# A hybrid decoder layer on one Trainium2 core: the embedding projection goes between output projection and FFN, the kernel begins with the gate rows and the first columns by token halves, and the first FFN pair is computed by seven products too

## The chip, the cores and the metric

One NeuronCore of a Trainium2 chip runs the whole layer. The engines that matter here are TensorE (PE, with its weight loads PEld beside it), VectorE (DVE), ScalarE (ACT) and GpSimd (POOL); SyncE (SP) and ACT issue the DMAs. The metric is device time per execution in microseconds (us); lower is better.

## The reference

One layer on 1,024 tokens, width 1,024, everything float32:

```python
u = RMSNorm(x)
y = u @ w_in              # columns of three token mixers and of the merge gates
# A: gated DeltaNet, 4 heads (conv, decay, delta rule); B: mLSTM, 4 heads; C: native sparse attention, 8 heads
h = x + (sum_i sigmoid(gate_i(u)) * (mixer_i(y) @ w_branch[i])) @ w_out
r = h + (silu(n @ w_gate) * (n @ w_up)) @ w_down        # n = RMSNorm(h), 2,816 hidden channels
out = r + sigmoid(RMSNorm(r) @ w_ple_gate) * (p @ w_ple_proj)   # p: 256 values per token
```

Among the columns of `w_in` are 40 that give one scalar per head and token (decay, write strength, input and forget gate of A and B, the branch gates of C). They are called the gate rows below.

## The kernel before

**Precision.** A float32 product is three fp32r matmuls: each factor is split into `hi` (a rounding copy, by ACT) and `lo` (the rest, by DVE or POOL), and hi\*hi, hi\*lo and lo\*hi are summed in PSUM. So each weight has `whi` and `wlo`, the normed input `uhi`/`ulo`, the FFN's input `u2hi`/`u2lo`.

**Blocks.** `run_blocks` goes through a list of weight blocks of up to 1 MB (four tiles of 128x512) on TensorE. In the middle of block i, `following` issues the split of block i+1 (`halve`) and, on SP, the load of block i+2. There are four raw buffers and five of each split half, so a split of the next block can also wait until TensorE has let go of an older one. The scalar and vector work of the mixers runs as generators that are advanced between matmuls; `later(lag, ...)` puts a step that many microseconds of TensorE work further on. Every engine runs its instructions in one fixed order.

**Start.** A warm-up of 48 transposes, then the projection of p: 16 transposes `ptr` of p, 96 matmuls 128x512, 16 ACT copies `pp` and 16 stores to DRAM, where p's projection waits for the end of the kernel. Between these matmuls the normed x is transposed (`trx`, 64) and split into `uhi`, `ulo` (L320, L321). Then the block of the gate rows, 32 matmuls, then the gated DeltaNet's first head: query and key columns (96 matmuls), value and output-gate columns. The gate rows are transposed (`gtr`), and a chain of small steps makes the decays of A and the stabiliser of B from them (L653 on).

**Middle.** The rest of the in-projection beside the mixers' scans, attention, then the branch projections, which end in `merged`.

**Out projection** (`out_blocks`): eight blocks (token half, quarter of 256 columns), each row tile 24 matmuls with 256 moving columns; after the fourth quarter of a row tile `norm_after` normalises it, and `to_u2` transposes it into `u2hi`/`u2lo` (eight 128x128 pieces).

**FFN.** The 2,816 hidden channels are 11 pairs of 256. Pair 0 is done plainly: `gate` and `up` with 96 matmuls each, then `down(0)` with 96. Pairs 1 to 10 are done by seven products in place of eight (`seven(f)`): a gate and an up tile of 128 channels, as a 2x2 block matrix over channel kind and half of the width, times the 2x2 input over width and token half. That needs sums of weights (`sums`, DVE) and four sums of inputs T1 to T4. `ffn_combine(k)`, k = 0 to 3, makes the latter, each with 12 DVE operations of 128x512 (`uw` sums, `utT..l` remainders) and four ACT copies `utT..h`; they are due 8 us of TensorE work apart, behind the last `norm_after`.

**Gate at the end** (`ple_blocks`): like the out projection, 768 matmuls of 256 columns.

Of the kernel before, what the change touches and what calls it, by code (L numbers as in the profile page):

```python
# [11 lines left out]
F32 = mybir.dt.float32  # L12
F32R = mybir.dt.float32r
# [20 lines left out]
NORM_AT = [1, 3]  # L34
TRX_AT = [0, 0, 1, 1, 3, 3, 4, 4, 7, 8, 9, 10, 11, 12, 13, 14]
FOLLOW_AT = 12
CONST_AT = 2
# [23 lines left out]
def _constants():  # L61
# [44 lines left out]
    add("rowscale", np.where((m % 64 >= 4) & (m % 64 < 8), -1.0, 1.0))  # L106
# [30 lines left out]
def _blocks(w_in, w_branch, w_out, w_ffn_in, w_ffn_out, w_ple_gate, w_ple_proj):  # L137
# [5 lines left out]
    out.append(w_ple_proj.reshape(2, P, 2, 512).transpose(1, 2, 0, 3).reshape(P, -1))  # L143
    rows = np.zeros((D, 256), w_in.dtype)
    for dst, src, n in ((0, 2048, 4), (4, 4108, 4), (8, 2052, 4), (12, 4104, 4), (16, 5392, 24)):
        rows[:, dst:dst + n] = rows[:, 64 + dst:64 + dst + n] = w_in[:, src:src + n]
    cols(rows, (0, 256))
# [21 lines left out]
    for c in range(4):  # L169
        cols(w_out, (256 * c, 256))  # L170
    for i in range(NFP):
        if i == 0:
            cols(w_ffn_in, (0, 256))
            cols(w_ffn_in, (DFF, 256))
        else:
            for c in (256 * i, 256 * i + P):
                g, u = (_rows(w_ffn_in[:, o:o + P]) for o in (c, DFF + c))
                out.append(np.concatenate([t.reshape(P, -1) for t in (g[:, :4], u[:, :4], u[:, 4:], g[:, 4:])], 1))
        out.append(w_ffn_out[256 * i:256 * i + 256].reshape(2, P, 2, 512).transpose(1, 2, 0, 3).reshape(P, -1))
    for c in range(4):  # L180
        cols(w_ple_gate, (256 * c, 256))
# [3 lines left out]
def _layout(x, p, rel_bias, norm_mix, w_in, conv_w, gdn_a_log, gdn_dt_bias, gdn_norm, mlstm_b_i, mlstm_b_f,  # L185
# [17 lines left out]
    chan.append(rb)  # L203
    o["chan"] = np.concatenate(chan, 1)
# [10 lines left out]
       "pe": (74, 64), "rowb": (138, 1)}  # L215
# [12 lines left out]
class Trunk:  # L228
    def __init__(self, ctx, tc, x, p, w, relb, chan, rowp, wcmp, c128, cset, c33, out, dbg=None):
# [169 lines left out]
    def run_blocks(self, blocks, rate, both=0, first=None, fetch=None):  # L399
# [21 lines left out]
        def halve(i):  # L421
            if i < n:
# [4 lines left out]
                for t in parts:  # L427
                    hi = self.wpool.tile([P, 512], F32R, tag="whi", name="whi", bufs=W_BUFS[1])
                    lo = self.wpool.tile([P, 512], F32R, tag="wlo", name="wlo", bufs=W_BUFS[1])
                    nc.scalar.activation(hi, t, AF.Copy)  # L430
                    eng = nc.vector if len(blocks[i]) == 2 and len(self.wsplit[i]) % 2 < both else nc.gpsimd
                    eng.tensor_tensor(lo, t, hi.bitcast(F32), OP.subtract)  # L432
# [1685 lines left out]
```

## Time and profile before

| | |
|---|---|
| median of 3 runs | 2327.62 us (2327.32 to 2328.61) |
| profiled execution: time | 2327.02 us |
| its span | 2325.2 us, mean granted clock 0.994 |
| TensorE busy | 2263.7 us, 97% |
| VectorE, ScalarE, GpSimd busy | 57%, 37%, 31% |

The span is the time between the first and the last instruction that the profiler saw; the 1.8 us between it and the execution's own time is launch and end. TensorE's 3% of idle time is what any wait has cost; the rest is matmuls, transposes and their clock. The projection of p, which the table does not show apart, is among the first 62 us.

### The profile page before, as it was taken

Reading aid. Unit: us, or ns where it says so; the run is one execution under the profiler, and the core shown is the slowest. Engines: PE = TensorE matmul, PEld = TensorE weight load, DVE = VectorE, ACT = ScalarE, POOL = GpSimd, SP = SyncE. Lnnn points to the kernel's source line nnn. Section 1 sums busy time; section 2 is a strip of 40 time slices with the busy share of each in tenths; the row PEclk is TensorE's granted clock in tenths of the full one; section 3 lists DMA queues with packets and bytes.
Section 4 is the critical chain, followed back from the end, with each engine's and each line's share of the span. In section 5 each row is a group of like instructions: output and inputs, shape, how many; then the busy total and the mean of one; then the engine's idle time right before and its main releaser. Section 6 shows DMA issues by size and latency. Waiting matters only on the chain.

```text
span 2325.2 us, 34431 instructions
## 1 busy us (share of the span) xinstructions
PE 2263.7 (97%) x12800; PEld 1836.2 (79%) x12800; DVE 1332.0 (57%) x3096; ACT 852.3 (37%) x1832; POOL 729.1 (31%) x616
## 2 busy tenths in 40 slices
PE   7999999999999999999999999999999999999999
PEld 6777878788778996677667778987888888888899
DVE  6456564645223446888883456586555555555594
ACT  6423232423332335555553222453222222222362
POOL 2343334433231123322122151214334444344411
PEclk9999999999999999999999999999999999999999
DMA  6131312111222132111103553311111111111144
GB/s 235 47 104 37 98 37 89 58 50 52 82 69 75 47 111 87 64 46 37 46 33 130 199 183 122 119 55 46 55 50 51 51 54 50 50 50 55 55 139 130
DMA packets 121887, 183.05 MB, mean 79 GB/s; under 512 B 25275, under 2 KB 47204, under 8 KB 121720
## 3 DMA queue, kind: packets, MB, share of 16 engines
q1 hardware_dynamic: 121432, 180.72, 23.6%
q8 instruction: 101, 1.65, 0.3%
q14 instruction: 66, 0.54, 0.1%
q10 hardware_dynamic: 288, 0.14, 0.0%
HBM read 149.04 MB, written 31.76 MB: 78 GB/s over the span
## 4 chain that ended last, share of the span: by engine, by line
PE 84%; DVE 10%; issue 2%; ACT 2%; DMA 1%; POOL 1%; SPq 0%; ACTq 0%; POOLq 0%; DVEq 0%
PE mm L243 68%; PE nso L243 3%; PE ptr L251 2%; PE S L243 2%; DVE P L1525 1%; PE mops L243 1%; PE gks L243 1%; PE gram L243 1%; PE gpu L243 1%; DVE P L1514 1%; POOL wlo L432 0%; DVE uw L1825 0%; DVE kT L824 0%; DVE xn L1778 0%; PE u2tr L251 0%
## 5 line engine op out<-in xcount | busy, mean ns | idle before, releaser
L432 POOL TENSOR_TENSOR wlo<-wraw,whi 128x512 fp32r<-128x512 f32 x334 | 443.8, 1335 | 1021.8 <-ACT whi L430 790.0
L243 PE MATMUL mm<-u,whi 128*128 128x512 f32 x1888 | 628.5, 408 | 3.6 <-ACT mg L1654 2.0
L430 ACT ACTIVATE whi<-wraw 128x512 fp32r<-128x512 f32 x408 | 255.8, 630 | 417.3 <-PE mm L243 335.7
L243 PEld LDWEIGHTS mm<-u,whi 128*128 128x128 f32 x1888 | 345.1, 190 | 76.8 <-issue 5.2
L243 PE MATMUL mm<-u,wlo 128*128 128x512 f32 x928 | 374.2, 403 | 3.1 <-POOL wlo L432 3.1
L243 PEld LDWEIGHTS mm<-u,wlo 128*128 128x128 f32 x928 | 175.8, 189 | 41.0 <-POOL wlo L432 3.5
L1896 DVE TENSOR_TENSOR fc<-fc,mm 128x512 f32<-128x512 f32 x140 | 95.2, 686 | 156.1 <-PE mm L243 156.1
L1937 DVE TENSOR_TENSOR h<-h,mm 128x512 f32<-128x512 f32 x176 | 118.6, 684 | 58.6 <-PE mm L243 57.3
L243 PE MATMUL mm<-whi,ahi 128*128 128x512 f32 x352 | 140.2, 398 | 2.0 <-ACT utT4h L1819 2.0
L243 PE MATMUL mm<-whi,alo 128*128 128x512 f32 x352 | 141.4, 402 | 0.0
L243 PE MATMUL mm<-wlo,ahi 128*128 128x512 f32 x352 | 140.2, 398 | 0.0
L432 POOL TENSOR_TENSOR wlo<-ws,whi 128x512 fp32r<-128x512 f32 x60 | 85.0, 1416 | 153.6 <-ACT whi L430 153.6
L243 PE MATMUL mm<-u2hi,whi 128*128 128x512 f32 x304 | 121.2, 399 | 0.0
L243 PE MATMUL mm<-u2lo,whi 128*128 128x512 f32 x304 | 120.9, 398 | 0.0
L243 PE MATMUL mm<-u2hi,wlo 128*128 128x512 f32 x304 | 120.4, 396 | 0.0
L1520 ACT ACTIVATE P<-P,n_ng 128x640 f32<-128x640 f32 (+7 forms) x128 | 92.8, 727 | 53.5 <-DVE n_ng L1518 53.0
L430 ACT ACTIVATE whi<-ws 128x512 fp32r<-128x512 f32 x60 | 37.8, 630 | 171.4 <-DVE h L1937 126.1
L251 PE MATMUL ptr<-ident,P 128*128 128x128 f32 x528 | 88.6, 281 | 8.2 <-DVE P L1525 7.5
L243 PE MATMUL mm<-whi,u 128*128 128x256 f32 x512 | 94.2, 283 | 0.0
L251 PEld LDWEIGHTS ptr<-ident,P 128*128 128x128 f32 x528 | 60.8, 141 | 40.4 <-DVE P L1525 13.1
L432 DVE TENSOR_TENSOR wlo<-wraw,whi 128x512 fp32r<-128x512 f32 x74 | 64.5, 871 | 46.0 <-ACT whi L430 46.0
L243 PEld LDWEIGHTS mm<-whi,alo 128*128 128x128 f32 x352 | 66.6, 189 | 18.8 <-DVE alo L1853 3.2
(506 smaller groups left out, 4995.2 us busy)
## 6 DMA issues: line engine op xcount, KB each, us to landing
wraw<-in_w_dram SPq DMA_DIRECT2D x408, 256.0 KB, 2.6
mgs<-mg SPq DMA_DIRECT2D x48, 256.0 KB, 2.2
mgld<-mgs SPq DMA_DIRECT2D x48, 256.0 KB, 5.4
xt<-in_x_dram SPq DMA_DIRECT2D x8, 512.0 KB, 6.0
xt<-in_x_dram SPq DMA_DIRECT2D x32, 128.0 KB, 3.4
sg<-pps SPq DMA_DIRECT2D x32, 128.0 KB, 3.3
out_dram<-sg SPq DMA_DIRECT2D x32, 128.0 KB, 2.4
pps<-ppst SPq DMA_DIRECT2D x8, 256.0 KB, 2.0
```

The source lines that it names most:

```text
L243: return self.nc.tensor.matmul(out, lhsT, rhs, start=start, stop=stop).ins
L251: self.nc.tensor.transpose(out, in_, self.ident[:n, :n])
L430: nc.scalar.activation(hi, t, AF.Copy)
L432: eng.tensor_tensor(lo, t, hi.bitcast(F32), OP.subtract)
L1514: nc.vector.tensor_tensor_reduce(pt[:, farw:nk], sp2[:, farw - cut:nk - cut], near[g][:, n % 2], 1.0, -3e38, OP.add, OP.max, mx[:, n, 1:2])
L1520: nc.scalar.activation(pts[i][:, :nk], pts[i][:, :nk], AF.Exp, bias=ng[:, i:i + 1], accum_out=sm[:, g, i % 2:i % 2 + 1])
L1525: nc.vector.tensor_scalar(pts[i][:, :nk], pts[i][:, :nk], sm[:, g, i % 2:i % 2 + 1], gate[:, g, i % 2:i % 2 + 1], OP.mult, OP.mult)
L1896: nc.vector.tensor_tensor(t, x, ps, OP.add)
L1937: nc.vector.tensor_tensor(self.h[tt][s], self.h[tt][s], ps, OP.add)
```

## The change

**Start.** The projection of p is no longer there, nor the 1 MB weight block of the gate rows: their 40 columns come by a DMA of their own on ACT's queue (`wgr`), are split by ACT and DVE into `wg` (104 columns, hi and lo side by side) and are multiplied in `first_block`, between the transposes of x. That block is the first head's query and key block, ordered by token halves: transposes and gate rows of half 0, query and key columns of half 0, transposes and gate rows of half 1, query and key columns of half 1.

**Out projection and last gate.** `wide_blocks` replaces `tok_block`: the token tile is held, 512 weight columns move; a block is half the width and half the columns, and eight blocks remain. The sum with x is written into x's tile.

**Projection of p.** Its loads (`load_p`) and transposes (`prep_p`) go out with the last out block, its matmuls stand between out projection and FFN, row tile by row tile.

**FFN pair 0.** `first_three(f)` for both f, then `last_four(f)` for both f, then `down(0)`. The weight block of a tile is loaded and split twice, once for each part. Three of the seven products need no T: B11, B21, B22 are plain pieces of the input.

**End.** The last tile's gate is finished in two halves.

```diff
+    def wide_blocks(self, u, evac, key, then=None):
...
+                    for k, (wh, wl) in enumerate(wb):
+                        uh, ul = u(4 * kh + k, tt)
+                        self.mm(ps, uh, wh, kh == 0 and k == 0, False)
+                        self.mm(ps, uh, wl, False, False)
+                        self.mm(ps, ul, wh, False, kh == 1 and k == 3)
+                    if kh == 1:
+                        evac(c, tt, ps)
+                    if then and kh and c:
+                        then(tt)
+                    self.passed(2.56)
...
+        return [(gen_for(c, kh, _HALF[hf]), (key, c, kh)) for hf in range(2) for c in range(2) for kh in range(2)]
...
-    def gates_block(self):
+    def first_block(self, evac):
...
+            trx(0)
+            trx(0)
+            gate_rows(0, 2)
+            self.norm_x(2)
+            self.norm_x(3)
             for hf in range(2):
...
+                        if hf == 0 and ct == 1 and kc > 4:
+                            trx(1)
...
+                    if hf == 0 and ct == 1:
+                        gate_rows(1, 3)
+                        self.load_gains()
+                        self.flags.add("rows")
+                    if hf == 1 and ct == 0:
+                        self.following()
...
+        def then(tt):
+
+            if tt == 4:
+                self.load_p()
+            elif tt > 5:
+                self.prep_p(tt - 6)
...
+        def sums_b(raw):
+            a11, a21, a22, _ = raw
+            s1, s2 = self.l2("ws1"), self.l2("ws2")
+            nc.vector.tensor_tensor(s1, a21, a22, OP.add)
+            nc.vector.tensor_tensor(s2, s1, a11, OP.subtract)
+            yield s2
...
+        def first_three(f):
+            def gen(wb):
...
+                nc.scalar.activation(c1, product(0, "B11"), AF.Copy)
+                yield
+                g0 = add(c1, product(1, "B21"))
+                nc.scalar.activation(g0, g0, AF.Silu)
+                yield
+                nc.scalar.activation(t7, product(2, "B22"), AF.Copy)
...
+        def last_four(f):
...
+                add(t2, product(0, "T2"), t2)
+                yield
+                t3 = add(t2, product(1, "T3"))
...
+                p5 = product(2, "T1")
...
+                add(t3, product(3, "T4"), t3)
...
             if i == 0:
-                blocks.append((self.chan_block(self.u2c, gate, halves_first=True), None))
-                blocks.append((self.chan_block(self.u2c, up, halves_first=True), None))
+                blocks += [(first_three(f), ("ffn", f), sums_a) for f in range(2)]
+                blocks += [(last_four(f), ("ffn", f), sums_b) for f in range(2)]
...
-                    t = self.s2("pp") if s else self.ppst[tt // 2][:, (tt % 2) * 512:(tt % 2) * 512 + 512]
+                    t = self.l2("pp")
                     nc.scalar.activation(t, ps, AF.Copy)
                     nc.sync.dma_start(self.pp[tt, :, s * 512:s * 512 + 512], t)
...
-                blocks = [(self.ple_proj_block(), None), (self.gates_block(), None)]
+                blocks = []
                 for h in range(4):
-                    blocks += self.gdn_blocks(h)
+                    blocks += self.gdn_blocks(h, h == 0)
```

How this moves instructions shows best in the order of three engines. In these lists a row is one instruction or a run of like ones: line of the file, operation, result and operands, size, count; lines are those of the file before and after, which differ. First TensorE from the program's start, before and then after (`warm`: warm-up, `ptr`: transposes of p, `pThi`/`pTlo`: p's halves, `trx`: transposes of x, `u`: its halves, `wg`: columns of the gate rows):

```order
L251 MATMUL warm<-ident 128x128 x48
L251 MATMUL ptr<-ident,pt 128x128 x16
L243 MATMUL mm<-whi,pThi 128x512
L243 MATMUL mm<-wlo,pThi 128x512
L243 MATMUL mm<-whi,pTlo 128x512
L243 MATMUL mm<-whi,pThi 128x512
L243 MATMUL mm<-wlo,pThi 128x512
L243 MATMUL mm<-whi,pTlo 128x512
L251 MATMUL trx<-ident,xt 128x128 x8
```

```order
L249 MATMUL warm<-ident 128x128 x48
L249 MATMUL trx<-ident,xt 128x128 x12
L241 MATMUL mm<-u,wg 104x512 x2
L249 MATMUL trx<-ident,xt 128x128 x4
L241 MATMUL mm<-u,wg 104x512 x2
```

The transposes of x and the gate rows stand where the projection of p stood. Second, ACT around the combinations, from the last copy of group k = 0 to the first of group k = 2 (`whi`: weight splits, `pp`: copies of p's projection out of PSUM, `sil`: pair 0's gate, `ws`: a sum of weights), before and after:

```order
L1819 ACTIVATE utT4h<-uw 128x512
L430 ACTIVATE whi<-wraw 128x512
L1858 ACTIVATE sil<-mm 128x512 x2
L430 ACTIVATE whi<-wraw 128x512 x2
L1819 ACTIVATE utT1h<-uw 128x512
L1819 ACTIVATE utT3h<-uw 128x512
L1819 ACTIVATE utT2h<-uw 128x512
L1819 ACTIVATE utT4h<-uw 128x512
L1858 ACTIVATE sil<-mm 128x512
L1819 ACTIVATE utT1h<-uw 128x512
```

```order
L1889 ACTIVATE utT4h<-uw 128x512
L2110 ACTIVATE pp<-mm 128x512 x6
L1889 ACTIVATE utT1h<-uw 128x512
L1889 ACTIVATE utT3h<-uw 128x512
L1889 ACTIVATE utT2h<-uw 128x512
L1889 ACTIVATE utT4h<-uw 128x512
L2110 ACTIVATE pp<-mm 128x512 x3
L431 ACTIVATE whi<-wraw 128x512
L2110 ACTIVATE pp<-mm 128x512
L431 ACTIVATE whi<-ws_14692 128x512
L2110 ACTIVATE pp<-mm 128x512 x3
L431 ACTIVATE whi<-wraw 128x512 x2
```

Thirteen of the sixteen copies of p's projection now stand behind the first combination, seven of them and four weight splits between the second and the third (whose `utT1h` is the row that follows). Third, DVE from the end of the last combination (k = 3) on (`h`: sums of the down projection, `alo`: pair 0's activation, `ws`: sums of weights, `fc`: sums of the products), before and after:

```order
L1825 TENSOR_TENSOR uw<-u2hi,u2lo 128x512
L1820 TENSOR_TENSOR utT2l<-uw,utT2h 128x512
L1837 TENSOR_TENSOR uw<-uw 128x512
L1862 TENSOR_TENSOR sil<-sil,mm 128x512
L1937 TENSOR_TENSOR h<-h,mm 128x512
L1820 TENSOR_TENSOR utT4l<-uw,utT4h 128x512
L1937 TENSOR_TENSOR h<-h,mm 128x512
L1853 TENSOR_TENSOR alo<-sil,ahi 128x512
```

```order
L1895 TENSOR_TENSOR uw<-u2hi,u2lo 128x512
L1890 TENSOR_TENSOR utT2l<-uw,utT2h 128x512
L1907 TENSOR_TENSOR uw<-uw 128x512
L1890 TENSOR_TENSOR utT4l<-uw,utT4h 128x512
L1972 TENSOR_TENSOR ws_15102<-wraw 128x512
L1973 TENSOR_TENSOR ws_15103<-ws_15102,wraw 128x512
L1975 TENSOR_TENSOR wraw<-wraw 128x512
L1956 TENSOR_TENSOR fc<-fc,mm 128x512
```

Before, pair 0's own results stand among the combinations; now the weight sums of `last_four(0)`, which the products with T2, T3, T1 and T4 need, stand behind the last of them.

## Rows read from the trace of the kernel before

**Rows 1.** The page's head and its busy times: busy us, share of the span, instructions.

```profile
span 2325.2 us, 34431 instructions
PE 2263.7 (97%) x12800; PEld 1836.2 (79%) x12800; DVE 1332.0 (57%) x3096; ACT 852.3 (37%) x1832; POOL 729.1 (31%) x616
```

**Rows 2.** Busy time by stretch: start and end of the stretch, its length, busy us and instructions of each engine, granted clock, DMA share, GB/s. The stretches are: projection of p and gate rows; rows' transposes and half of the first query and key block; its other half; the rest of the norms and the combinations; the tail of `down(0)`; a piece of the later FFN; the last gate; the tail.

```profile
13.94:62.54 48.60, 42.16 (x209) 33.25 (x209) 29.48 (x63) 30.56 (x54) 11.17 (x13) 0.96 0.60 207
62.54:81.30 18.76, 15.90 (x81) 12.43 (x81) 10.17 (x37) 7.29 (x17) 10.02 (x10) 0.91 0.18 57
81.30:92.50 11.20, 11.20 (x50) 9.04 (x49) 2.48 (x6) 3.94 (x9) 4.45 (x5) 1.00 0.04 12
1526.00:1584.00 58.00, 54.01 (x236) 43.21 (x235) 53.43 (x103) 30.57 (x67) 9.58 (x6) 0.97 0.14 47
1584.00:1601.40 17.40, 17.40 (x70) 13.92 (x69) 13.52 (x20) 1.73 (x3) 2.55 (x2) 0.90 0.09 31
2100.00:2200.00 100.00, 100.00 (x429) 80.08 (x428) 53.42 (x72) 29.79 (x49) 42.31 (x32) 1.00 0.17 56
2255.00:2321.10 66.10, 66.10 (x551) 65.90 (x550) 34.89 (x62) 20.29 (x42) 14.29 (x10) 1.00 0.51 159
```

**Rows 3.** Waits between 1420 and 1600 us, TensorE's: engine, line, what it waited for; us in total, times, longest.

```profile
PE u2tr L251 <- DVE u2lo L321: 3.9, 2, 2.0
PEld mm L243 <- ACT utT4h L1819: 2.5, 1, 2.5
```

**Rows 4.** TensorE by operation between 13.94 and 62.54 us: busy us, mean ns of one (they overlap), idle before and what ended it.

```profile
L251 PE MATMUL trx<-ident,xt 128*128 128x128 f32 x64 | 10.0, 292 | 1.7 <-DVE u L321 1.7
L243 PE MATMUL mm<-u,whi 128*128 128x512 f32 x32 | 8.1, 401 | 1.5 <-ACT pp L1987 1.4 <-DVE whi L628 0.2
L251 PE MATMUL ptr<-ident,pt 128*128 128x128 f32 x16 | 2.8, 288 | 4.0 <-DVE pTlo L318 2.7 <-DMA pt<-in_p_dram 1.3
```

**Rows 5.** Timeline of the start: start us, duration, engine, line, operation, result and operands, count, idle before.

```profile
9.64 1.42 DVE L577 TENSOR_SCALAR xt<-xt,rsq_ynr 128x1024 f32<-128x1024 f32 x2
11.80 4.96 POOL L432 TENSOR_TENSOR wlo<-wraw,whi 128x512 fp32r<-128x512 f32 x4 [10.28 <-ACT whi L430]
13.14 1.19 DVE L297 SCALAR_TENSOR_TENSOR rsq_tnr<-rsq_tnr,nr_ssqx 128x2 f32<-128x2 f32 x1
25.75 1.26 ACT L320 ACTIVATE u<-trx,chan 128x512 fp32r<-128x512 f32 x2
26.46 0.75 DVE L321 SCALAR_TENSOR_TENSOR u<-trx,chan,u 128x512 fp32r<-128x512 f32 x1 [1.53 <-ACT u L320]
```

**Rows 6.** Timeline of the gate rows' chain, the same columns (`gaterows`: their evacuation, `gm`: their transposed values, `mtr`: a transposition of B's chain).

```profile
62.54 0.45 PE L653 MATMUL gtr<-ident,gaterows 40*128 40x40 f32 x8
62.65 0.78 ACT L619 ACTIVATE gaterows<-mm,rowbias,c 104x512 f32<-104x512 f32 x1 [0.25 <-PE mm L243]
67.87 0.23 DVE L670 TENSOR_TENSOR g_tmp<-g_tmp,coef 128x64 f32<-128x64 f32 x1
74.83 0.22 PE L251 MATMUL mtr<-ident,m_crow 32*128 32x32 f32 x1 [2.86 <-DVE m_tmp L737]
```

**Rows 7.** DVE by operation from 1514.75 to 1583.92 us: busy us, mean ns, idle before.

```profile
L1825 DVE TENSOR_TENSOR uw<-u2hi,u2lo 128x512 f32<-128x512 f32 x16 | 12.6, 820 | 0.0
L321 DVE SCALAR_TENSOR_TENSOR u2lo<-u2tr,chan,u2hi 128x128 fp32r<-128x128 f32 x32 | 9.7, 345 | 2.1 <-ACT u2hi L320 2.0
L1760 DVE TENSOR_TENSOR h<-xt,mm 128x256 f32<-128x256 f32 x4 | 1.7, 417 | 0.7 <-PE mm L243 0.7
```

**Rows 8.** Timeline from the out projection's last quarter to the first `seven`, the same columns as rows 5.

```profile
1514.75 0.42 DVE L1760 TENSOR_TENSOR h<-xt,mm 128x256 f32<-128x256 f32 x1 [0.72 <-PE mm L243]
1515.96 0.16 DVE L1775 SCALAR_TENSOR_TENSOR na_ms<-na_ssq 128x1 f32<-128x1 f32 x1 [0.79 <-ACT xn L1773]
1517.69 0.88 DVE L1778 TENSOR_SCALAR xn<-h,rsq_yna 128x512 f32<-128x512 f32 x2
1529.17 2.55 DVE L321 SCALAR_TENSOR_TENSOR u2lo<-u2tr,chan,u2hi 128x128 fp32r<-128x128 f32 x9
1540.06 0.68 DVE L1825 TENSOR_TENSOR uw<-u2hi,u2lo 128x512 f32<-128x512 f32 x1
1548.49 0.63 ACT L430 ACTIVATE whi<-wraw 128x512 fp32r<-128x512 f32 x1 [1.53 <-PE mm L243]
1549.67 1.36 DVE L1820 TENSOR_TENSOR utT4l<-uw,utT4h 128x512 fp32r<-128x512 f32 x1 [0.98 <-ACT utT4h L1819]
1552.14 1.86 POOL L432 TENSOR_TENSOR wlo<-wraw,whi 128x512 fp32r<-128x512 f32 x1 [1.65 <-ACT whi L430]
1552.77 1.78 DVE L1825 TENSOR_TENSOR uw<-u2hi,u2lo 128x512 f32<-128x512 f32 x1
1558.20 0.68 DVE L1825 TENSOR_TENSOR uw<-u2hi,u2lo 128x512 f32<-128x512 f32 x1
1558.80 0.69 DVE L1820 TENSOR_TENSOR utT2l<-uw,utT2h 128x512 fp32r<-128x512 f32 x1
1583.31 0.68 DVE L1820 TENSOR_TENSOR utT4l<-uw,utT4h 128x512 fp32r<-128x512 f32 x1
1601.39 0.40 PE L243 MATMUL mm<-u2hi,whi 128*128 128x512 f32 x1
```

**Rows 9.** Granted clock behind the combinations; columns as in rows 2 (the clock is the third number from the end).

```profile
1583.50:1590.00 6.50, 6.50 (x23) 5.19 (x22) 6.50 (x12) 0.41 (x1) 0.00 (x0) 0.74 0.02 4
```

More of the change, by code (lines that the diff above doesn't have):

```diff
@@ L33 @@
 MG_ATT = 10
[L34 to L37, printed above, removed]
 WARM = 48
@@ L427, in halve, with part @@
                 for t in parts:
[L428 to L432, printed above, removed]
-                    self.wsplit[i].append((hi, lo))
+                    part(i, self.wsplit[i], t)
+        def part(i, to, t):
+            hi = self.wpool.tile([P, 512], F32R, tag="whi", name="whi", bufs=W_BUFS[1])
+            lo = self.wpool.tile([P, 512], F32R, tag="wlo", name="wlo", bufs=W_BUFS[1])
+            nc.scalar.activation(hi, t, AF.Copy)
+            eng = nc.vector if len(blocks[i]) == 2 and len(to) % 2 < both else nc.gpsimd
+            eng.tensor_tensor(lo, t, hi.bitcast(F32), OP.subtract)
+            to.append((hi, lo))
         self.raw, self.wsplit = {}, {}
@@ L453, in run_blocks @@
             first()
-        halve(0)
-        load(1)
+        if first:
+            to = self.wsplit[0] = []
+            self.split_first = lambda: part(0, to, self.raw[0][len(to)])
+        else:
+            halve(0)
+            load(1)
         if fetch:
@@ L1878, in sums, with products, product @@
             yield s2
+        def products(wb):
+            def product(n, b):
+                ps = self.ps("mm", "mm")
+                w = wb[n]
+                for k in range(4):
+                    wh, wl = (t[:, k * P:k * P + P] for t in w)
+                    uh, ul = self.ub[b][k]
+                    self.mm(ps, wh, uh, k == 0, False)
+                    self.mm(ps, wh, ul, False, False)
+                    self.mm(ps, wl, uh, False, k == 3)
+                self.passed(2.56)
+                return ps
+            return product
@@ new lines, in last_four, with gen @@
+        def last_four(f):
+            def gen(wb):
+                product = products(wb)
+                t2, g0, t7 = begun.pop(f)
+                add(t2, product(0, "T2"), t2)
+                yield
+                t3 = add(t2, product(1, "T3"))
+                nc.vector.tensor_tensor(t7, t7, t2, OP.add)
+                yield
+                p5 = product(2, "T1")
+                add(t7, p5, t7)
+                u1 = add(t3, p5)
+                nc.scalar.activation(t7, t7, AF.Silu)
+                yield
+                nc.vector.tensor_tensor(t7, t7, u1, OP.mult)
+                add(t3, product(3, "T4"), t3)
+                nc.vector.tensor_tensor(t3, t3, g0, OP.mult)
+                put(f, 0, t3)
+                put(f, 1, t7)
+                yield
+            return gen
@@ L1894, in add @@
-                def add(x, ps, to=None):
-                    t = to if to is not None else self.l2("fc")
-                    nc.vector.tensor_tensor(t, x, ps, OP.add)
-                    return t
+                product = products(wb)
                 c1 = self.l2("fc")
```

281 lines of the change are left out of this document (148 added, 133 removed).

## The prediction

> **What bounds the kernel now.** I read the page first. TensorE is busy for 2263.7 of 2325.2 us [rows 1], so a change counts by what it takes from TensorE's work and by where it leaves TensorE waiting. Then the stretches, for the price of that work where nothing else holds it: in the later FFN 429 matmuls of 512 columns take 100.00 us, 0.2331 us each, and in the last gate 551 of 256 columns take 66.10 us, 0.1200 us each [rows 2]. Then the two places that the change rewrites. At the start, from 13.94 to 62.54 us, TensorE is busy for 42.16 of 48.60 us, and part of that at a lower clock: 0.96 on the mean [rows 2]. Around the combinations DVE is busy for 53.43 of 58.00 us beside TensorE's 54.01 [rows 2], and yet TensorE's own waits there are small, 3.9 and 2.5 us [rows 3]: the 192 matmuls of gate and up (44.8 us) cover the combinations just about. That is the cover that the change takes off, so I worked out that place instruction by instruction.
>
> **The start.** Removed: 96 matmuls, 22.4 us at 0.2331, and 16 transposes `ptr`, which with the four waits around them are 2.8 busy and 4.0 idle [rows 4]. The new path, step by step. The third and fourth x tiles come from the norm that before ran beside POOL's weight remainders, where a 128x2 operation took 1.19 us [rows 5]; those remainders come later now, so that I put the first transposes with their x tiles at 14.5 us. Then ACT bounds the transposes and gate rows of half 0: eight splits `u` of 0.63 (1.26 for two) [rows 5] and four weight splits of the same size among them, 7.6 us, with two more steps of pipeline (DVE's 0.75 [rows 5] and the matmuls) 9.6, to 24.1 us. Query and key columns of half 0: 48 matmuls, 11.2 us [rows 2], and 1.3 for transposes among them, to 36.6. Transposes and gate rows of half 1 at ACT's pace, six of eight groups left, 6.0, to 42.6; evacuation 0.78 [rows 6], so `gtr` at 43.4 instead of 62.54. From `gtr` the old block's 48 matmuls with the gate rows' chain took 18.76 us [rows 2], with TensorE waiting 2.86 us for the chain at 74.83 [rows 6]; the same chain stands beside the last 48 matmuls now, to 62.2. The next block's remainders come later in the block than before and stand on POOL among the chain's operations: 3.0 us, between nothing and POOL's 4.96 for four [rows 5]. The block ends at 65.2 instead of 92.5: **27.3 us earlier**, bounds 24 (every wait repeats and x arrives 3 us late) and 29.5 (remainders hidden). 22.4 + 1.8 of it is only moved.
>
> **Middle.** The order of TensorE's work and of the mixers' steps is the same from there on, so nothing: the waits travel with it.
>
> **Out projection and last gate.** 768 matmuls of 256 columns (92.2 us) become 384 of 512 (89.5): 2.7 us each, **-5.4** for both stages. That holds because TensorE has no other wait there: 66.10 of 66.10 busy [rows 2]. The Trainium skill ("TensorE: Matmul & The Clock Gate", section "Back-to-back issue gap") gives an isolated gap of N/2.4 + 2.5 ns, which would make 218.4 ns of two narrow and 215.8 of a wide one and 1.0 us of the 2.7; the trace's pitches differ from both figures and go ahead.
>
> **End.** One operation of 256 columns more, 0.417 [rows 7]: **+0.4**.
>
> **Projection of p and pair 0.** I count from S, the sum of the last out quarter's first tile (1514.75 [rows 8]). Before, the first combination starts at S+25.3 (1540.06), the last ends at S+69.2 (1583.31 + 0.68), and the first product of `seven(2)` starts at S+86.6 (1601.39) [rows 8]. After:
> - DVE gains before the first combination four `pTlo` and three sums of weights, 7 x 0.60 (the step from 1558.20 to 1558.80 [rows 8]) = 4.2, wider sums with x, 1.1 (four at 0.68 [rows 8] instead of 0.417 [rows 7]), and loses a weight remainder, 0.6: S+30.0.
> - Group k = 0 took 11.0 us (1540.06 to 1549.67 + 1.36), 0.98 of it a wait for `utT4h`, which stood on ACT behind a weight split that waited 1.53 us for TensorE [rows 8]. That split is gone from there, an ordinary hand-over of 0.2 stays: 10.2, to S+40.2. Group 1: 12 x 0.60 and a hand-over, to 47.5.
> - TensorE begins the projection of p about S+14 and stops at its ninth product (S+25): five PSUM buffers, three copies `pp` ahead of the combinations, the fourth behind `utT4h` of group 0. So products 9 to 16 run from S+39.9 to S+51.1.
> - On ACT two weight splits stand ahead of group 2's `utT1h`, and they need buffers that TensorE frees with the sixteenth product. That is the same pattern as at 1548.49 [rows 8], longer: `utT1h` at S+53.6 instead of 50.5. DVE, which does nothing out of order, idles 3.1 us. Group 2 ends at S+60.0.
> - Then three weight sums, one sum of a product and group 3, 16 operations, 9.7, and 1.1 for one collision with POOL (below): the last combination ends at **E = S+70.8**.
> - Only then come the sums of weights for the products with T2, T3, T1, T4: two on DVE (1.2), ACT 0.63, POOL 1.3, hand-overs: T2's product at S+74.1. The 72 matmuls of `first_three` (16.8 us) fit between 51.1 and 74.1 with 6 us to spare, so TensorE waits.
> - 8 products of 12 matmuls, 22.4; 2.2 until the last activation is split; `down(0)`, 96 matmuls, 22.4; and after such stops a piece at half clock: the stretch 1583.5 to 1590 has a granted clock of 0.74 [rows 9], so 6.5 x 0.26 = 1.7. `seven(2)` at S+122.8: **+36.2**.
>
> By matmuls alone this would be +22.4 - 5.6 (168 for 192) = +16.8; the other 19.4 are TensorE waiting for the combinations.
>
> **One price is open:** what POOL's remainders cost DVE. All of pair 0's are POOL's now, eight tiles of them beside the combinations. One `uw` took 1.78 us beside a POOL remainder of 1.86, where 0.68 is usual [rows 8]: 1.1 more. But `uw` is 0.82 on the mean over 16 [rows 7], so most meet none. I take one collision in the chain that counts; bounds none and six. The Trainium skill ("SBUF — State Buffer", section "Who interferes with whom") says that DVE and GpSimd share a pair of ports under an exclusive lock; the 1.78 agrees, and if every remainder held DVE up for its whole length, the second rival below would be the forecast.
>
> **Sum** against the profiled execution's 2327.02 (0.6 under the median of the three runs, so it needs no shift): -27.3 + 36.2 - 5.4 + 0.4 = +3.9, **2331 us**.
>
> **Rivals.**
> - *POOL blocks DVE* (slower): five more collisions of 1.1 in the chain, +6: 2337. For it: all eight remainders stand on POOL, and the 128x2 operation of 1.19 shows how small operations suffer [rows 5]. Against: the mean of 0.82. It decides from 1.5 us on (2332.3 is the edge below). Chance 0.24.
> - *The combinations run through* (faster): DVE's work from S to E, added up by the rows' pitches, is 57.4 us: 48 operations of the combinations (29.0), 32 `u2lo` at 0.283 (2.55 for nine [rows 8]), twelve others of 512 columns (7.2), four sums with x (2.4), and four norms (small operations from 1515.96 to 1517.69 and 0.88 of scaling each [rows 8], less what overlaps: 9.7). With only the two waits of 0.79 for ACT's squares [rows 8] E is S+59.0, T2's product S+62.3, no stop of the clock, `seven(2)` at S+109.3, +22.7: 2317. For it: before, DVE worked at 92% in this stretch [rows 2]. Against: 12 us of such losses before too (57 of work in 69.2), and the order on ACT, which is fixed. Chance 0.24.
> - *The start gains only 20*: x tiles or the gate rows' columns come late and the chain's waits repeat per half; 2338. Against: the first x was normed at 9.64 [rows 5]. Chance 0.05.
> - *The wide matmuls give only 1.0 us a stage*: 2334. Against it the two pitches of the same kernel. Chance 0.05.
>
> **How the numbers follow.** The likeliest case has 0.42 and its own range of 2324 to 2334, from the start's bounds. A measurement of this kernel can tell about 0.2% from no change, that is 4.7 us: faster is under 2323, slower over 2332.3. Faster: the second rival and 0.05 of the likeliest, 0.29. Same: 0.29 of the likeliest. Slower: its last 0.08, the first rival, and the two small ones, 0.42. The range reaches from the second rival with the best start (2317 - 2) to the first with a start of 24 (2337 + 3): 2315 to 2340.
>
> **What would show it.** Right: `gtr` near 43 us; the first block's end near 65; the out projection's matmuls at 0.233; TensorE idle behind the eighth product of p's projection until the first combination's last copy, some 15 us; a second idle piece of some 6 us ahead of the first product with T2; a lower clock behind both; T2's weight sums behind `utT4l` of k = 3 on DVE. Wrong: TensorE running through the projection of p (then the order on ACT does not hold the copies up), or waits in the mixers' part that were not there before, which I put at nothing, or combinations of clearly more or less than 41 us.

## The result and the profile after

| kernel | median, us | beside the kernel before |
|---|---|---|
| before | 2327.47 | |
| changed | 2341.62 (2340.79 to 2347.51) | 1.0076, 95% interval 1.0062 to 1.009 |

By the medians the change is slower by 14 us (by the ratio it would be 18), which is 1.6 us beyond the upper end of the forecast's range (2340). The first trace of the changed kernel is its slowest execution:

```profile
span 2345.7 us, 32721 instructions
PE 2263.3 (96%) x12008; PEld 1794.0 (76%) x12008; DVE 1339.0 (57%) x3071; ACT 855.2 (36%) x1824; POOL 736.0 (31%) x621
```

Against [rows 1] TensorE has 792 matmuls fewer and is as long busy, more of it at a lower clock (0.988 granted on the mean, before 0.994). The working below uses a second trace of the same kernel (span 2342.4), which is nearer to the median; the large stops have the same length in both. By stretch, columns as in [rows 2] (from the last transposes `gtr` to the end of the first block's matmuls; the second block's first part; its stops at the transposes of keys and queries; the projection of p; pair 0 before `down(0)`; the last gate):

```profile
43.74:64.90 21.16, 17.10 (x79) 12.98 (x80) 13.97 (x47) 7.52 (x19) 7.00 (x7) 0.92 0.07 26
64.90:78.00 13.10, 12.02 (x52) 9.37 (x52) 5.94 (x5) 4.34 (x7) 8.53 (x9) 1.00 0.17 60
78.00:92.00 14.00, 10.19 (x44) 7.90 (x43) 7.66 (x7) 7.21 (x29) 0.26 (x2) 0.88 0.00 1
1504.20:1546.20 42.00, 28.49 (x127) 22.34 (x126) 35.90 (x84) 25.61 (x63) 3.93 (x3) 0.88 0.31 113
1546.20:1595.10 48.90, 41.62 (x169) 32.06 (x168) 33.44 (x48) 21.59 (x38) 18.71 (x15) 0.93 0.32 108
2239.40:2337.00 97.60, 95.05 (x425) 75.59 (x423) 61.19 (x138) 45.12 (x107) 23.07 (x15) 1.00 0.45 149
```

TensorE is idle for 13.5 of 42.0 us in the projection of p and for 7.3 of 48.9 in pair 0, where [rows 2] has 4.0 idle of 58. Its waits at the start (40 to 100 us; engine, line, what it waited for, total, times, longest):

```profile
PE ktr L249 <- DVE gq L894: 3.1, 1, 3.1
PE mm L241 <- POOL wlo L433: 1.1, 1, 1.1
PE ktr L249 <- DVE kT L894: 0.7, 1, 0.7
```

and between 1490 and 1620 us, where [rows 3] had 3.9 and 2.5:

```profile
PE mm L241 <- ACT pp L2110: 9.4, 1, 9.4
PE mm L241 <- ACT whi L431: 6.3, 2, 5.9
```

The timeline shows what stood ahead on the same engine (columns as in [rows 5]; rows of ACT, DVE and PE; `xk`: copy of the first head's keys out of PSUM, `kT` and `gq`: the convolved keys and queries):

```profile
65.88 0.63 ACT L923 ACTIVATE decay<-decay 128x512 f32<-128x512 f32 x1 [1.76 <-POOL decay L922]
69.39 0.63 ACT L923 ACTIVATE decay<-decay 128x512 f32<-128x512 f32 x1 [2.35 <-POOL decay L922]
70.45 0.58 ACT L876 ACTIVATE xk<-mm 128x512 f32<-128x512 f32 x1
71.06 1.08 DVE L889 TENSOR_SCALAR kT<-xk,chan 128x1024 f32<-128x1024 f32 x1 [5.98 <-ACT xk L876]
78.14 1.23 DVE L894 SCALAR_TENSOR_TENSOR kT<-ct,kT 128x1024 f32<-128x1024 f32 x1 [1.13 <-ACT ct L893]
85.13 1.22 DVE L894 SCALAR_TENSOR_TENSOR gq<-ct,gq 128x1024 f32<-128x1024 f32 x1 [1.13 <-ACT ct L893]
...
1531.78 0.63 ACT L1889 ACTIVATE utT4h<-uw 128x512 fp32r<-128x512 f32 x1 [1.78 <-DVE uw L1907]
1532.31 2.53 ACT L2110 ACTIVATE pp<-mm 128x512 f32<-128x512 f32 x5
1532.94 0.80 PE L241 MATMUL mm<-whi,pThi 128*128 128x512 f32 x1 [9.43 <-ACT pp L2110]
1549.78 0.63 ACT L431 ACTIVATE whi<-wraw 128x512 fp32r<-128x512 f32 x1 [2.04 <-DMA wraw<-in_w_dram]
1550.96 1.37 DVE L1890 TENSOR_TENSOR utT1l<-uw,utT1h 128x512 fp32r<-128x512 f32 x1 [5.48 <-ACT utT1h L1889]
```

At the start, ACT's copy `xk` stands behind two exponentials of the decays, which wait for POOL; the product was done at about 65, the copy comes at 70.45, and DVE's convolution starts after an idle time of 5.98. In the late place, p's copies stand behind `utT4h` of the first combination, as forecast. The clock fell as well: from within each of the two late stops (they ended at 1532.94 and 1570.63) TensorE was granted 1.2 of its 2.4 GHz,

```profile
1526.60:1536.80 10.20, 3.85 (x9) 3.12 (x10) 9.02 (x16) 6.22 (x12) 0.00 (x0) 0.50 0.30 115
1567.50:1574.30 6.80, 3.53 (x8) 2.32 (x9) 3.19 (x5) 4.47 (x9) 3.64 (x3) 0.50 0.13 42
```

That is 17 us at half clock, in 7.4 of which TensorE worked.

### The profile page after: what moved, and what is told of

Same layout as the page of the kernel before. It is cut to its first block, busy times and chain, and to the rows that moved or that the text cites. A ratio compares the mean times of both kernels' runs of the same rounds, so it can differ in the third digit from the quotient of the medians.

```text
span 2345.7 us, 32721 instructions
## 1 busy us (share of the span) xinstructions
PE 2263.3 (96%) x12008; PEld 1794.0 (76%) x12008; DVE 1339.0 (57%) x3071; ACT 855.2 (36%) x1824; POOL 736.0 (31%) x621
## 4 chain that ended last, share of the span: by engine, by line
PE 81%; DVE 10%; issue 4%; ACT 2%; DMA 1%; POOL 1%; SPq 0%; DVEq 0%; ACTq 0%; POOLq 0%
PE mm L241 66%; PE nso L241 3%; PE ptr L249 2%; PE S L241 2%; DVE P L1592 1%; PE mops L241 1%; POOL wlo L433 1%; PE gks L241 1%; PE gram L241 1%; DVE kT L891 1%; PE gpu L241 1%; DVE P L1581 1%; DVE xn L1849 0%; DVE u2lo L319 0%; DVE rsq_tna L307 0%
## 5 line engine op out<-in xcount | busy, mean ns | idle before, releaser
L1956 DVE TENSOR_TENSOR fc<-fc,mm 128x512 f32<-128x512 f32 x152 | 103.2, 686 | 156.6 <-PE mm L241 156.4
L2061 DVE TENSOR_TENSOR xt<-xt,mm 128x512 f32<-128x512 f32 x176 | 118.6, 685 | 60.5 <-PE mm L241 59.2
L433 POOL TENSOR_TENSOR wlo<-ws,whi 128x512 fp32r<-128x512 f32 x66 | 92.9, 1408 | 173.4 <-ACT whi L431 170.6
L241 PE MATMUL mm<-u2hi,wlo 128*128 128x512 f32 x264 | 104.0, 394 | 0.9 <-POOL wlo L433 0.9
L241 PE MATMUL mm<-u2hi,whi 128*128 128x512 f32 x264 | 104.5, 396 | 0.1
L241 PE MATMUL mm<-u2lo,whi 128*128 128x512 f32 x264 | 104.5, 396 | 0.0
L249 PEld LDWEIGHTS ptr<-ident,P 128*128 128x128 f32 x528 | 60.5, 140 | 40.0 <-DVE P L1592 13.2
L241 PEld LDWEIGHTS mm<-whi,alo 128*128 128x128 f32 x352 | 66.3, 188 | 18.9 <-DVE alo L1922 3.4
```

The lines of the kernel that those rows point to most:

```text
L241: return self.nc.tensor.matmul(out, lhsT, rhs, start=start, stop=stop).ins
L249: self.nc.tensor.transpose(out, in_, self.ident[:n, :n])
L1956: nc.vector.tensor_tensor(t, x, ps, OP.add)
L2061: nc.vector.tensor_tensor(self.h[tt][s], self.h[tt][s], ps, OP.add)
```

## Experiments

Times are medians beside runs of the kernel before on the same chip, which was 2325.3 to 2327.6 in them.

**The wide matmuls alone**, in the kernel before.

> The kernel before with only the 512-wide out projection and last gate (and the last tile in two halves). By the pitches of the trace of before (0.1200 and 0.2331 us): -2.7 for each stage and +0.4 at the end, -5.0, about 2322.5. By the isolated gap that the Trainium skill gives (TensorE: Matmul & The Clock Gate, section Back-to-back issue gap): -1.0 a stage, -1.6 with the end, about 2325.9. By what the trace of after shows of the two stages (out projection 97.3 us without p's transposes for 99.8, last gate 98.0 for 99.1, tail 5.4 for 4.1): -2.3, about 2325.2.

2323.03, ratio 0.9978 (0.9968 to 0.9987): 4.1 us, nearest to the first of the three sums. The two stages, before and then with the wide matmuls:

```profile
1424.40:1524.20 99.80, 96.54 (x811) 96.12 (x810) 58.39 (x149) 39.64 (x96) 23.41 (x17) 1.00 0.39 127
2222.00:2321.10 99.10, 97.45 (x809) 96.21 (x807) 66.03 (x170) 47.21 (x124) 20.62 (x15) 1.00 0.48 151
```

```profile
1425.40:1523.30 97.90, 95.28 (x427) 76.20 (x427) 56.06 (x134) 40.40 (x97) 23.27 (x17) 1.00 0.39 129
2216.70:2314.50 97.80, 95.35 (x425) 75.56 (x423) 61.92 (x138) 45.14 (x107) 22.54 (x15) 1.00 0.44 148
```

The stages gave 1.9 and 1.3 us instead of 2.7 each, and the tail took 0.8, together 2.4: that is the third sum, and the total's nearness to the first is partly luck. The larger part of this trace's gain is not in these stages: from S to `seven(2)` it takes 82.0 us instead of 86.6, because the wait for `utT4h` and the half-clock stretches beside pair 0 are missing (no half clock from 1000 to 2300 us). No run shows whether the wide matmuls took them away or this execution merely lacked them.

Even the 1.9 and 1.3 are not clear of what one execution differs from another. A later trace of narrow matmuls (the kernel before with another order at the start, last paragraphs of this section) has the same two stages in

```profile
1418.50:1516.50 98.00, 95.24 (x811) 94.81 (x810) 57.70 (x148) 39.29 (x95) 22.80 (x17) 1.00 0.40 130
2213.10:2310.70 97.60, 95.92 (x809) 94.72 (x807) 65.98 (x170) 47.06 (x124) 20.63 (x15) 1.00 0.49 153
```

which is as fast as with wide ones. From one narrow matmul to the next it took 0.120 and 0.121 us on the mean in the two stages of the first trace, 0.118 and 0.119 in this one; from one wide matmul to the next 0.236 and 0.237, not the 0.2331 of the later FFN.

**Pair 0 as before**, in the changed kernel.

```diff
-                blocks += [(first_three(f), ("ffn", f), sums_a) for f in range(2)]
-                blocks += [(last_four(f), ("ffn", f), sums_b) for f in range(2)]
+                blocks.append((self.chan_block(self.u2c, gate, halves_first=True), None))
+                blocks.append((self.chan_block(self.u2c, up, halves_first=True), None))
...
```

(The rest of the edit puts the weights of pair 0 and the steps behind its products as in the kernel before.)

> The changed kernel with pair 0 as before (gate and up, 192 matmuls, no products with T). If TensorE's second stop and its clock come from the products with T waiting for the last combination and its weights: the stop of 5.8 us, 3.4 of half clock and the split of pair 0 go, 24 matmuls (5.6 us) come back, the stop at the ninth product of p's projection stays: about 2338. If the combinations are not what holds TensorE there, only the 5.6 us of matmuls count: about 2347.

2337.57. The stop ahead of T2 is gone, the stop at the ninth product is there, and 24 matmuls more take 4 us less time:

```profile
PE mm L245 <- ACT pp L2124: 10.1, 1, 10.1
```

**Combinations later**, pair 0 by seven products.

```diff
-                self.later(NORM_LAG + COMBINE_LAG * k, lambda k=k: self.ffn_combine(k))
+                self.later(NORM_LAG + 9.0 + 5.8 * k, lambda k=k: self.ffn_combine(k))
```

> The changed kernel with the combinations made due 9 us of TensorE work later and 5.8 apart instead of 8, so that ten of p's copies stand ahead of the first combination on ACT instead of three. If the order on ACT makes the stop at the ninth product (9.4 us and the half clock behind it): the stop goes, the first product with T2 comes 10 to 12 us earlier, about 2330. If the combinations' own length on DVE decides alone, TensorE only waits later, ahead of T2, for as long: about 2341.

2340.43. The stop at p's projection fell from 9.4 to 1.8 and that stage took 33 us instead of 42, but only 1 to 3 us of time came out. TensorE's waits in this place and a piece of DVE's timeline:

```profile
PE mm L241 <- ACT whi L431: 5.2, 1, 5.2
PE mm L241 <- ACT utT2h L1889: 2.8, 1, 2.8
...
1560.80 4.05 DVE L1895 TENSOR_TENSOR uw<-u2hi,u2lo 128x512 f32<-128x512 f32 x3
1564.88 1.65 DVE L1900 TENSOR_TENSOR uw<-uw 128x512 f32<-128x512 f32 x1
1566.57 1.64 DVE L1902 TENSOR_TENSOR uw<-uw 128x512 f32<-128x512 f32 x1
```

DVE idles less (3.9 us instead of 9.6 from the first combination to the last), but it now runs beside POOL's weight remainders. Of its 48 operations of the combinations 11 overlap one of POOL and take 1.43 on the mean, 37 take 0.68: 8.2 us are lost, where the changed kernel lost 1.7 on four. There POOL had worked while DVE idled.

**Decays of the first head on DVE** instead of POOL (`own = nc.vector if h == 0 else nc.gpsimd`).

> The changed kernel with the two additions and two products on the first head's decays on DVE instead of POOL, where they stand between the remainders of the second weight block. If ACT's late copy of the first head's keys (it stands behind the decays' exponentials) holds up the convolution: the copy comes some 4 us earlier, TensorE's waits for the convolved keys and queries (0.7 and 3.2 us) shrink to under 1 and the half clock behind them may go: 2336 to 2338. If the convolution itself is the limit, with four more operations on DVE ahead of it, nothing changes: 2341.6.

2341.4, no change. `xk` comes at 69.97 instead of 70.45: it still stands behind both exponentials, which now wait for DVE. The edit replaced the engine and left the order, so it does not test the order.

**The changed kernel again.**

> The changed kernel unaltered, for a second trace of it. The first trace lies 6 us over the median of the other executions (2347.5 and 2341.6). If that is the clock alone, the stops of TensorE are the same here (9.4 us at the ninth product of p's projection, 5.8 ahead of T2, 3.2 ahead of the transposes of the convolved queries) and the half-clock stretches are shorter by some 10 us: 2341. If stops differ from one execution to another, some of these are gone.

2343.25. The stops of 9.4, 5.8 and 3.1 are the same; the half-clock stretches within the span sum to 47.9 us instead of 54.7. The profiled execution took 3.2 us less, about half of that difference.

**Convolutions ahead of the decays.** The generator of the first head waits for the keys and issues both convolutions ahead of the decays (its later pause is 8 instead of 12).

> The changed kernel with the first head's decays issued behind its convolutions, so that ACT's copy of the keys no longer stands behind the decays' exponentials. If that copy (70.5 us, its product done at 64) starts the convolution late: it comes at about 64.7, the convolution ends 5 to 6 us earlier, the stop of 3.2 us ahead of the queries' transposes and the half clock behind it go: 2336 to 2337. If TensorE only meets the next late thing (the decays, now 14 us later, or the remainders on POOL): 2341.

2342.51. `xk` comes at 66.22, 4.2 earlier, but ACT's tanh of the keys then stands behind the decays' exponentials (DVE idles 4.28 ahead of its last step at 78.98), and TensorE waits 3.7 for the keys and 0.6 for the queries, instead of 0.7 and 3.1:

```profile
PE ktr L249 <- DVE kT L894: 3.7, 1, 3.7
PE ktr L249 <- DVE gq L894: 0.6, 1, 0.6
```

The wait moved on by one place in ACT's order.

**Pair 0 as before and the combinations 16 us later.**

> The changed kernel with pair 0 as before and the combinations due 16 us later, behind all copies of p's projection on ACT. In the run with plain pair 0 TensorE stopped for 10.1 us at p's ninth product and 10.2 us of half clock followed, 15 us together; nothing needs the combinations before the first product of pair 1, some 67 us of matmuls later. If the order on ACT made that stop: 2322 to 2325, level with the kernel before or a little faster. If DVE's work itself holds TensorE: the stop moves to pair 1's first product with T2 and the time stays about 2337.

2324.32, ratio 0.9989 (0.9979 to 0.9998): 13 us under plain pair 0 alone, where only the time of the combinations differs. The projection of p in this trace:

```profile
1501.00:1530.00 29.00, 26.71 (x129) 20.91 (x128) 17.02 (x54) 21.06 (x56) 2.85 (x2) 1.00 0.44 164
```

It took 29 us at full clock instead of 42, and the stop did not come back at the first product with T2: the order on ACT had made it.

**The same with the convolutions first.**

> The last two edits together: pair 0 as before, the combinations behind p's copies, the first head's decays behind its convolutions. If both mechanisms hold and lie in different stretches, they add: 2317 to 2320, faster than both kernels. If the convolution's stop only moves: as the run with the combinations alone.

2321.69: 2.6 less, not the 4 to 7 expected. The stop had moved, as above.

**The same with a pause**, so that the decays stand behind both tanh too.

```diff
+        if h == 0:
+            yield from self.need(("g", h, "k"))
+            kT = self.conv_silu(st.pop("k"), 4 + h, "kT")
+            yield
+            qT = self.conv_silu(st.pop("q"), h, "gq")
+            yield from self.pause(14.0)
         dps = self.row_bcast([c[:, :, h] for c in self.cumhl], "gcb")
...
```

(Further down the first head leaves out its two convolutions and the pause of 12, which stood behind the decays.)

> The kernel with plain pair 0 and the combinations 16 us later, and with the first head's decays behind both convolutions on DVE and ACT (in the first try ACT's tanh of the keys still stood behind the decays, and the stop moved from the queries to the keys: 3.7 us). If the order of keys' copy, tanh and decays on ACT makes TensorE's stops of 0.7 and 3.2 us ahead of the transposes: both under 0.5, with the half clock behind them 4 to 5 us less than without the edit (2324.3): 2319 to 2320. If the decays, now last, come late for the products of keys and queries: a new stop there and 2323 to 2325.

**2312.28, ratio 0.9934 (0.992 to 0.9949): faster than both kernels**, and 12 under the run without the edit, more than twice the 4 to 5 expected. TensorE's waits from 60 to 180 us:

```profile
PE gpu L245 <- DVE gvn L1103: 2.1, 1, 2.1
PE ktr L253 <- ACT g_junk L954: 1.8, 1, 1.8
```

The stops at keys and queries are gone, and also a wait of 3.1 to 3.5 for a weight remainder on POOL at 141 us, which the kernel before has at 163. The transposes also stand 18 matmuls later in TensorE's order, so that the edit changes two orders at once. The trace of the same edit in the changed kernel (below) tells them apart in part; DVE's last steps on keys and queries are

```profile
74.53 1.23 DVE L894 SCALAR_TENSOR_TENSOR kT<-ct,kT 128x1024 f32<-128x1024 f32 x1 [1.12 <-ACT ct L893]
81.52 1.23 DVE L894 SCALAR_TENSOR_TENSOR gq<-ct,gq 128x1024 f32<-128x1024 f32 x1 [1.13 <-ACT ct L893]
```

3.6 us earlier than in the changed kernel (78.14 and 85.13). There TensorE, without its two stops, would have come to the queries' transposes at 82.7, just when the queries are now done: the earlier convolution by itself nearly covers both stops. What the later transposes add to the rest of the 12 us was not tested.

**The combinations' first sums on POOL** (the 16 `uw` of two SBUF operands), with the later combinations.

> The changed kernel with the later combinations (2340.4) and the 16 sums uw of two SBUF operands of the combinations on POOL, 12 operations of a group on DVE become 8. If POOL's operations hold DVE's up for their whole length (as the Trainium skill states of two-operand operations in SBUF: State Buffer, Who interferes with whom), DVE gains 16 x 0.6 and loses 16 x 1.1 to 1.3: the combinations end 8 to 11 us later, 2347 to 2351. If a collision is as rare as the mean of 0.82 for uw before suggested, they end up to 9 us earlier: 2331 to 2334.

2344.5, 4 slower than without; it lies between the two expectations, nearer to the first. POOL's and DVE's groups:

```profile
L1895 POOL TENSOR_TENSOR uw<-u2hi,u2lo 128x512 f32<-128x512 f32 x16 | 24.2, 1536 | 18.4 <-DVE u2lo L319 18.4
L1890 DVE TENSOR_TENSOR utT3l<-uw,utT3h 128x512 fp32r<-128x512 f32 x4 | 6.0, 1499 | 0.0
```

19 of DVE's 32 operations overlap one of POOL and take 1.63 on the mean, 18 us lost, and DVE waits 6.7 us for POOL's sums besides. From first to last the combinations take 56.4 us instead of 47.6. A collision costs 0.9 us, near the 1.1 of the first rival; it costs nothing where DVE waits anyway.

**Pair 1's first three products ahead of T2 as well.**

> The changed kernel, pair 0 still by seven products, with the three products without T of pair 1 also ahead of the first product with T (weights of pair 1's tiles then loaded twice too), and the combinations due 12 us later. 22.4 + 33.6 us of matmuls stand between the last out block and T2 instead of 39.2. If the combinations' lateness is all that the change loses in this place: no stop at p's ninth product, under 2 us ahead of T2, no half clock: 5.6 less than the run with plain pair 0 and the later combinations (2324.3), 2318 to 2320. If DVE, with three more sums of weights for each of two more tiles, only falls further behind: a stop of 5 us or more remains and the time is 2328 to 2335.

2342.31: no gain, and outside both expectations. There is more plain work to cover the combinations, but TensorE stops for ACT again (4.9, 4.1 and 2.4), DVE meets 16 collisions (11 us), and the last combination ends 13 us later, counted from S:

```profile
PE mm L241 <- ACT fc L1993: 5.1, 2, 4.9
PE mm L241 <- ACT whi L431: 4.1, 1, 4.1
PE mm L241 <- ACT pp L2113: 2.4, 1, 2.4
```

**The order at the start, alone and with others.** The edit with the pause, in four more kernels. With pair 1's products ahead:

> The run before with the decays behind both convolutions at the start. The two places are 1400 us apart: 4 to 5 us less than the run before it, 2314 to 2316, if both mechanisms hold; no less than that run if the stop at the start only moves on.

In the changed kernel:

> The changed kernel with one edit: the first head's decays behind both convolutions. If the order at the start is the part that the forecast's start term missed: 9 to 12 us under the changed kernel (2341.6 to 2343.3), 2330 to 2333, with the late stops of 9.4 and 5.8 unchanged. If the gain seen with plain pair 0 needed the later combinations too: 2338 or more.

In the kernel before:

> The kernel before with the same edit. Its queries and keys were convolved without a stop of TensorE; only the wait for a weight remainder on POOL at 163 us (3.1 us and a half-clock stretch, 4 to 5 together) is shared with the changed kernel. If the changed kernel's start loses by the order of its own: nothing to 5 us here, 2322 to 2327. If the edit repairs something that both kernels have: 9 to 12 here too, 2315 to 2318, and the forecast's start term was right.

In the changed kernel with later combinations:

> The changed kernel with pair 0 by seven products, the later combinations (2340.4) and the decays behind the convolutions. The start's edit is worth 9 to 12 and the places are far apart: 2328 to 2331. Against the run with plain pair 0 and the same two edits (2312.3) this says what the seven products cost here when both orders on ACT are mended: 16 to 19 us, if DVE's and POOL's collisions beside the combinations (8 us in the trace of that run) and the wait ahead of T2 stay.

And the kernel before once more:

> The kernel before with the decays behind the convolutions, for a second trace. The first trace (2323.9) lies 6 us over the median of its other executions (2317.9) and gives the edit 3 to 4 us; the median gives it 9.7. If the clock at the start decided (10.2 us of half clock at 15 us in the first trace): the stops are the same and this trace is nearer to 2318, with the edit worth 7 to 10 by the trace too. If the median of five was a lucky one: 2322 to 2324 again.

| kernel | without the edit | with it |
|---|---|---|
| before | 2327.5 | 2317.90, second time 2318.14 |
| changed | 2341.6 to 2343.3 | 2330.07 |
| changed, combinations later | 2340.43 | 2327.71 |
| changed, pair 1's products ahead | 2342.31 | 2329.38 |
| changed, pair 0 plain, combinations later | 2324.32 | 2312.28 |

The first of these expectations (2314 to 2316) rested on a base that had come out 22 us higher; the edit gave 13. The kernel before gains 7 to 10 by the edit (ratios 0.9965 and 0.9969 against its own runs), the changed ones 11 to 13. So most of what the edit repairs lies in both kernels, and 2312.28 is only some 6 us under the kernel before with the same edit.

How far the changed kernel is ahead at the end of the branch projections is read from the first matmul of the out projection. In order: before, changed (second trace), before with the edit (second trace, span 2314.8), changed with the edit (span 2326.5):

```profile
1424.39 0.28 PE L243 MATMUL mm<-whi,mhi 128*128 128x256 f32 x1
1405.48 0.40 PE L241 MATMUL mm<-whi,mhi 128*128 128x512 f32 x1
1418.52 0.28 PE L243 MATMUL mm<-whi,mhi 128*128 128x256 f32 x1
1388.84 0.39 PE L241 MATMUL mm<-whi,mhi 128*128 128x512 f32 x1
```

Without the edit TensorE's work stands 18.9 us earlier in the changed kernel here, with it 29.7; at 125 us it is 21.5 and 26.5. By these traces the edit gives the changed kernel 4.2 us up to 125 us and takes 0.7 from the kernel before; the rest of its gain comes later, in both kernels, where the wait for POOL and several half-clock stretches fall away.

The seven products of pair 0 cost 15.4 us with both orders mended (2327.71 against 2312.28). The traces of these two kernels from S to `seven(2)`, seven products first:

```profile
1479.68:1601.57 121.89, 106.75 (x444) 83.58 (x443) 102.48 (x184) 56.60 (x120) 30.42 (x21) 0.93 0.30 102
1481.78:1588.07 106.29, 104.19 (x468) 83.34 (x467) 80.23 (x162) 50.89 (x110) 14.99 (x11) 1.00 0.28 97
```

TensorE idles 15.1 us instead of 2.1 and works 16.0 us at half clock instead of none, which costs about 8; the 24 matmuls saved give 5.6 back.

## Why the prediction was wrong

The step that failed is the middle: that the order stays the same there, "so nothing: the waits travel with it". The mechanisms of the other terms held, most of their sizes too; the sum was 10 us short by the medians. Against the second trace of the changed kernel, whose span is 17.2 us over that of before, the terms (forecast +3.9) are:

- **The start and the middle.** Up to the first block's end the forecast was right: its last matmul ends at 65.1 (65.2 forecast), 28 us earlier than before, and the first `gtr` is at 42.1 and 42.8 in the two traces (43.4). Then the second block lost 6 to 7 of the 28: ACT's copy of the keys behind the decays, the convolutions 5 us late, TensorE's stops of 0.7, 3.1 and 1.1, a half-clock stretch behind them. The kernel before has no stop there. Such "waits in the mixers' part that were not there before" were the prediction's own sign of being wrong. It had seen that the second block's remainders stand among the chain's operations on POOL and priced that at 3 us; what queues behind them on ACT it did not follow. With the out projection, p's eight transposes before that point included, S stands 21.3 us earlier, not 30.0: 8.7 of the miss of 13.3. The third rival ("the start gains only 20", 2338, chance 0.05) had about this size, but by late x tiles and by waits in the chain of the gate rows, which did not come.
- **How much of this loss is the change's own** stays open. The kernel before gained by the mended order too, and by the expectation for that run its 2317.90 says that the start term was right. By the medians the edit lessens the difference of the two kernels only from 14 to 12; by the ratios it goes from 1.0076 to 1.0013 / 0.9967 = 1.0046, 7 us less; by the traces it is 5.5 less in the spans and 10.8 (29.7 - 18.9) up to the out projection. Executions of one kernel differ by up to 10 us here. What belongs to the changed kernel alone is seen up to 125 us: the stops, which the other lacks, and 5 us that the edit gives (26.5 - 21.5).
- **In the pair of traces with the edit** the start is right: S stands 29.8 us earlier, the projection of p and pair 0 take +40.1, the last gate +0.2, the tail +1.2, together +11.7. The 7.8 that are left of the miss lie in pair 0's place and in the wide matmuls, whose gain in the last gate is absent, because the narrow ones are faster in that trace of before.
- **The projection of p and pair 0**: +38.5 for +36.2. Step by step: the first combination starts at S+29.6 (30.0 forecast), the first ends at 39.7 (40.2), TensorE's ninth product resumes at 39.5 (39.9), the last combination ends at 75.1 (70.8), T2 comes at 77.2 (74.1), and from there to `seven(2)` it takes 48.0 (48.7). The stop was 9.4 for some 15, since TensorE came to the ninth product at S+30 instead of S+25; the second was 5.8 for 6. What was too small is the way from the first combination to the last: products 9 to 16 took 13.2 us instead of 11.2, because they began with 3.9 us at half clock, which the forecast had only behind T2; and the late `utT1h` of group 2 had a second cause, a weight tile's DMA (2.04). The forecast's own steps for group 2 (47.5, twelve at 0.60 and a hand-over, 3.1 idle) add up to 57.9 and not to its 60.0; measured is 63.3.
- **The wide matmuls**: 1.9 and 1.3 us in the stages for 2.7 each, and less against the other trace of narrow ones; the 0.2331 was the pitch of another stage. In the changed kernel the last gate gave 1.3, and the tail took 1.3 for 0.4.
- **POOL's price**: one collision of 1.1 was taken, four were measured, 1.7 us. The prediction read from the mean of 0.82 that most `uw` meet none; over all 48 operations of the combinations before, ten met one, 5.0 us. The rival that POOL blocks DVE (the first in the list, though the prediction once calls it the second) did not come about in the changed kernel, whose DVE idled while POOL worked. It came where the idle time was taken away (8.2 us).
- **The second rival**, the combinations running through, is refuted by the traces: no edit brought the last one to S+59; the earliest of all runs with pair 0 by seven products is S+75.

The chances put 0.42 on slower. The 0.29 on "same" rested on a middle without loss, which the order of a few instructions decided.

## What to carry to other kernels

When work is moved ahead, follow the instructions that stand behind it on every in-order engine up to the next block, not only to the point where the moved work ends: in both places copies out of PSUM on ACT stood behind steps that waited for POOL or DVE, and TensorE stopped in the end. Before a cheaper algorithm replaces plain work, ask what that plain work covered: 24 matmuls saved (5.6 us) cost 15, because they and the rest had covered the vector engine's 41 us of combinations. Two mended orders were worth 12 us (at the start, most of it in the kernel before as well) and 13 (at the projection of p), with no matmul more or less. And try a mended order in the kernel before too: only the part of the gain that does not come there belongs to the change.

## What the runs showed of the hardware

TensorE's granted clock was 2.4 or 1.2 GHz. In the second trace of the changed kernel it fell within the stops: in the stop of 9.4 us (to 1532.94) from 1526.6 on, and 3.9 us of work behind the stop still ran at 1.2 GHz; behind the stop of 5.8 us it was 3.7, behind that of 3.1 us 3.0. If half of these is lost (an estimate), a stop's whole price was a fifth to a half more than its idle time. A DVE operation of two SBUF operands (128x512) takes 0.68 us alone and, beside a POOL operation, 1.1 to 1.6 on the mean of a trace and 1.8 at most; POOL's grow as well, from 1.29 to 1.54 on the mean, so that moving sums to POOL made the combinations longer. The last gate's 768 narrow matmuls and their transposes took 99.1 us in one execution and 97.6 in another, both at full clock.
